# Experts taken in order of load, in steps of one, two or four; shared expert in fp32, fourteen weight buffers, context work moved to layer borders

## The chip, the cores and the metric

One core of one Trainium2 chip runs the whole program as one launch. The metric is the device time of that launch in microseconds (us); smaller is better. The five engines are named as the profile names them: PE (matrix), DVE (vector), ACT (scalar), POOL and SP, the last of which here only issues DMA transfers.

## The reference, cut to what matters

The input x is 256 tokens of 1024 values, batch 1, all in fp32. A first block of two layers (neighbourhood attention with FFN, dilated attention with FFN) is followed by a second block: modulation vectors from `c` and `c_ctx` (called `ada`), a token mixer that also reads 256 context tokens, and a mixture of experts. The change works mostly on the last:

```python
scores = jax.nn.sigmoid(h @ router_w)                  # 256 tokens x 64 experts
...
_, idx = lax.top_k(sel, 8)                             # 8 experts for each token
wts = jnp.take_along_axis(scores, idx, axis=1)
wts = wts / jnp.sum(wts, -1, keepdims=True) * 2.5
...
hid = jax.nn.silu(xb @ w1[e]) * (xb @ w3[e])           # xb: the tokens of expert e
acc.at[tok].add(wt[:, None] * (hid @ w2[e]))
...
shared = (jax.nn.silu(h @ sw1) * (h @ sw3)) @ sw2      # all tokens
```

Each of w1, w3, w2 of an expert is 1024x256 (or 256x1024) in fp32, 1 MiB. There are 64 routed experts and one shared, so 195 MiB of weights if each is read once. The reference's own router, run on the inputs, gives loads (tokens per expert) of 81, 80 and 79 for the three largest and 55 for the next; of the 60 experts after the first four, the 32nd in order of load has 28.

## The kernel before

Up to the mixer, every weight is loaded by `wload` (L387) into a ring of fp32 buffers and split by `wsplit` into a high part `wh` (ACT, L404) and a low part `wl` (DVE, L413). PE then runs three matmuls for one (`yh,wh`, `yl,wh`, `yh,wl`; `proj_a`, `proj_b`). `post` (L548) ends each layer: squares, a sum of squares on PE (`c_base,big 128x1` matmuls), the norm, the residual sum, the next norm. Work on the context tokens and on `ada` is a generator that `beside` sets and `step` advances: the layers call `step` at places written by hand (once per pair of heads, three times at the end of `post`, PS = 3), so that PE gets independent matmuls there. A tile scheduler places all instructions by priority on each engine.

The experts start with `moe` (the shared expert, with split weights and a split input `xh`, `xl`), `route` (scores, top 8, position of each token in its expert's list) and `natural` (tokens turned round). Then `experts` (L2080) takes the routed ones in order of their numbers in pairs. An expert has CAP = 64 slots. One step (a pair) is `moe_in` (w1 in PE's columns 0 to 63 and w3 in 64 to 127 side by side, one expert after the other; 64 tokens `xe` against weights `w`), `moe_out` of the pair before (w2, `w,G`), `moe_slots` (`c_base,oh` and `gate,oh`), a part of the gather for the steps to come (`oh,hnh` and `oh,hnl`), `moe_hidden` and the `scatter` of the pair before (`P,yh` and `P,yl`). Experts with over 64 tokens get further blocks: after step 1, `route_more` counts them, NX = 3 are run after the 64 with weights loaded by an address from a register (`value_load`), and what is still over goes through a loop (`overflow`), which is empty on these inputs. So the kernel loads 3 + 67x3 = 204 MiB here, in 33 pairs and one single step.

The weights come through a ring of `w32` buffers on SP's DMA queue, nine deep from the shared expert on (MW = (9, 4)). A load is issued when its buffer is released by the last matmul that read it; a DMA of SP that waits holds up all behind it. `route_more` issues three of its own on that queue (`scr` twice, `idd`), behind the loads of the third pair.

Of the kernel before, what the change touches and what calls it, by code (L numbers as in the profile page):

```python
# [19 lines left out]
KT = D // 128  # L20
# [7 lines left out]

def _constants():
# [82 lines left out]
    c["ltm"] = lt  # L114
    return {k: np.ascontiguousarray(v, dtype=f) for k, v in c.items()}, mask8
# [3 lines left out]
MOEC = ["iota", "slot", "pidx", "jm", "ltm", "lt8"]  # L119
# [160 lines left out]
class Builder:  # L280
# [267 lines left out]
    def post(self, banks, g, xT, mul=None, perm=None, xnew=None, nxt=None):  # L548
# [20 lines left out]
        self.step(PS)  # L569
        return nxt  # L570

    def out_proj(self, name, oh, ol):
        banks = []
        for j in range(4):
            if j:
# [10 lines left out]
    def na_layer(self, xT, pre, **kw):  # L586
# [6 lines left out]
        for p in range(8):  # L593
            if p % 2 == 0:
# [11 lines left out]
                self.step()  # L606
# [40 lines left out]
        banks = self.out_proj("w_nao", oh, ol)  # L647
        return self.post(banks, self.vec["norm_mix_post0"], xT, **kw)

    def dil_layer(self, xT, pre, **kw):  # L650
# [8 lines left out]
        for p in range(8):  # L659
# [47 lines left out]
            self.step()  # L707
# [38 lines left out]
    def block1(self, xT, xT2, uh, ul):  # L746
# [6 lines left out]
        with self.psum(pc=2, pb=4), self.pool("bp"), self.pool("mp"):  # L753
            with self.pool("ap"), self.pool("lp") as lp:
                pre = self.norm_in(self.vec["norm_mix_pre0"])
                for h in (0, 1):
                    s = slice(4 * h, 4 * h + 4)
                    self.nc.sync.dma_start(xT[:, s, :], self.A["x"][:, s, :])
                    for kt in range(4 * h, 4 * h + 4):
                        pre[2](kt, xT[:, kt, :])  # L760
                self.beside(self.ctx_in(R), lp=lp, bp=None, tags=side)
                pre = self.na_layer(xT, pre, nxt=lambda: self.norm_in(self.vec["norm_ffn_pre0"]))
                self.step(99)
            with self.pool("ap"), self.pool("mr"), self.pool("lp"):
# [3 lines left out]
                pre = self.ffn_layer(xT, 0, pre, perm=(o, i), xnew=xT2, nxt=lambda: self.norm_in(self.vec["norm_mix_pre1"]))  # L768
# [5 lines left out]
            with self.pool("ap"), self.pool("mr"):  # L774
                with self.stream(tc.cur_priority, side):
                    self.load_consts(self.mr, "mixs")
                    self.ssd_ctx(R)
                    self.gla_ctx(R)
                self.ffn_layer(xT2, 1, pre, perm=(i, o), xnew=xT, nxt=lambda: self.ln_in(uh, ul))[3]()
        self.bp = None  # L780

    def ctx_in(self, R):
# [4 lines left out]
        uh, ul = (self.sb(self.lp, [128, KT, 256], t, F32R) for t in ("xh", "ul"))  # L787
        add, sums = self.ln_sums(self.lp, sq="ul")
# [1046 lines left out]
    def route(self, ps):  # L1835
# [47 lines left out]
        nc.vector.tensor_tensor(pos[:, :, 0:64], ps[:, 0:128].rearrange("p (t e) -> p t e", t=2), far, op=OP.add)  # L1883
# [6 lines left out]
        for tt in (0, 1):  # L1890
            nc.vector.tensor_scalar(gate[:, tt, 0:64], sc[:, tt, :], dn[:, 2 + tt:3 + tt], 2.5, op0=OP.mult, op1=OP.mult)
        return sel_

    def route_more(self, sel_):

        nc, mp, c, pos, gate = self.nc, self.mp, self.cst, self.pos, self.gate

        ptf = self.sb(mp, [96, 256], "ptf")
        gtf = self.sb(mp, [96, 256], "gtf")
        for dst, src in ((ptf, pos), (gtf, gate)):  # L1900
            ps = self.pst("pa")
            for tt in (0, 1):
                nc.tensor.transpose(ps[0:64, 128 * tt:128 * tt + 128], src[:, tt, 0:64], self.ident)
            nc.vector.tensor_copy(dst[0:64, :], ps[0:64, 0:256])
        ps = self.pst("pa")
        for tt in (0, 1):
            self.mm(ps[0:64, 0:1], sel_[tt], self.ones[:, 0:1], tt == 0, tt == 1)
        cnt = self.sb(mp, [64, 4], "cnt")
        for b in (1, 2, 3):
            nc.vector.tensor_scalar(cnt[:, b:b + 1], ps[0:64, 0:1], float(b * CAP) + 0.5, None, op0=OP.is_gt)  # L1910
        nc.vector.tensor_tensor(cnt[:, 0:1], cnt[:, 1:2], cnt[:, 2:3], op=OP.add)
        nc.vector.tensor_tensor(cnt[:, 0:1], cnt[:, 0:1], cnt[:, 3:4], op=OP.add)
# [3 lines left out]
        S = self.sb(mp, [64, 32], "S_")  # L1916
        W = self.sb(mp, [64, 32], "W_")
        t = self.sb(mp, [64, 32], "St")
        for b in (1, 2, 3):
            nc.vector.tensor_scalar(pre[:, b:b + 1], ps[0:64, 0:1], float(b - 1), None, op0=OP.add)  # L1920
            d = S if b == 1 else t
            nc.vector.tensor_scalar(d, c["jm"][0:64, :], pre[:, b:b + 1], cnt[:, b:b + 1], op0=OP.is_equal, op1=OP.mult)
            if b == 1:
                nc.vector.tensor_scalar(W, d, float(-CAP) - FAR, None, op0=OP.mult)
            else:
                nc.vector.tensor_tensor(S, S, t, op=OP.add)
                nc.vector.scalar_tensor_tensor(W, t, float(-b * CAP) - FAR, W, op0=OP.mult, op1=OP.add)

# [8 lines left out]
        for tt in (0, 1):  # L1937
            ps = self.pst("pa")
            self.mm(ps[:, 0:32], ptf[0:64, 128 * tt:128 * tt + 128], S, True, False)
            self.mm(ps[:, 0:32], one64, W, False, True)  # L1940
            self.mm(ps[:, 32:64], gtf[0:64, 128 * tt:128 * tt + 128], S, True, True)
            nc.vector.tensor_scalar(pos[:, tt, 64:96], ps[:, 0:32], FAR, None, op0=OP.add)
            nc.vector.tensor_copy(gate[:, tt, 64:96], ps[:, 32:64])
# [3 lines left out]
        nc.vector.tensor_copy(self.ids[:, 0:32], ps[0:1, 0:32])  # L1947
        nc.vector.tensor_scalar(self.ids[:, 32:33], ps[0:1, 32:33], float(-NX), 0.0, op0=OP.add, op1=OP.max)
# [4 lines left out]
    def gather_make(self, pos, n):  # L1953

        o = self.sb(self.gp, [128, 2, 4, CAP], "oh", F32R, bufs=2)
        for tt in (0, 1):
            self.nc.vector.tensor_tensor(o[:, tt, 0:n, :], self.cst["iota"][:, None, :].to_broadcast([128, n, CAP]),
                                         pos[:, tt, :].unsqueeze(2).to_broadcast([128, n, CAP]), op=OP.is_equal)
        return o, self.sb(self.gp, [128, KT, 4 * CAP], "xe", bufs=2)

    def gather_part(self, o, xe, n, q):

        w = CAP * n
        ps = self.pst("pa")
        for k in (0, 1):
            kt = 2 * q + k
            for x, h in enumerate((self.hnh, self.hnl)):
                for tt in (0, 1):
                    self.mm(ps[:, w * k:w * k + w], h[:, tt, 128 * kt:128 * kt + 128],
                            o[:, tt, 0:n, :].rearrange("p e s -> p (e s)"), x == 0 and tt == 0, x == 1 and tt == 1)  # L1970
# [6 lines left out]
    def moe_in(self, xe, i, ws):  # L1977

        pu = self.pst("pa")
        n = len(ws)  # L1980
        for b, (w1, w3) in enumerate(ws):
            o = slice(256 * b, 256 * b + 256)
            for kt in range(KT):
                l = xe[:, kt, CAP * (i + b):CAP * (i + b) + CAP]
                for a, w in ((0, w1), (64, w3)):
                    self.mm(pu[a:a + 64, o], l, w[:, 256 * kt:256 * kt + 256], kt == 0, kt == KT - 1)
# [19 lines left out]
    def moe_out(self, G, ws, gcol):  # L2006

        m = CAP * len(ws)
# [13 lines left out]
    def moe_slots(self, o, i, j, n):  # L2022

        nc = self.nc
        m = CAP * n
        ps = self.pst("pa")
        oh = [o[:, tt, i:i + n, :].rearrange("p e s -> p (e s)").bitcast(F32) for tt in (0, 1)]
        for tt in (0, 1):
            nc.tensor.transpose(ps[0:m, 128 * tt:128 * tt + 128], oh[tt], self.ident)
        for tt in (0, 1):  # L2030
            self.mm(ps[0:m, 256:256 + n], oh[tt], self.gate[:, tt, j:j + n], tt == 0, tt == 1)
        P = self.sb(self.gp, [128, 256], "P_", F32R, bufs=3)
        nc.vector.tensor_copy(P[0:m, :], ps[0:m, 0:256])
        gc = self.sb(self.gp, [128, 3], "gc", bufs=3)
        nc.vector.tensor_tensor_reduce(gc[0:m, 1:1 + n], ps[0:m, 256:256 + n], self.cst["b64"][0:m, 0:64 * n:64],
                                       scale=1.0, scalar=0.0, op0=OP.mult, op1=OP.add, accum_out=gc[0:m, 0:1])
        return P[0:m, :], gc[:, 0:1]
# [15 lines left out]
    def moe(self, hh, hl, acc, after):  # L2053

        nc, A, tc = self.nc, self.A, self.tc
        src = A["w_exp"][0]
        w1, w3, w2 = (self.wsplit(self.wload(src[i]), PSH[i], after, self.lp) for i in range(3))
        pg, pu = self.pst("pa"), self.pst("pa")
        self.proj_a(w1, hh, hl, pg)
        self.proj_a(w3, hh, hl, pu)  # L2060
        f = self.sb(self.gp, [128, 512], "us", bufs=2)
        s = f.rearrange("p (a b) -> p a b", a=2)
        nc.scalar.activation(f, pg, AF.Silu)
        nc.vector.tensor_tensor(f, f, pu, op=OP.mult)
# [243 lines left out]
```

## Time and profile before

| | us |
|---|---|
| median of 3 runs | 2001.54 (1997.59 to 2004.25) |
| the profiled execution: its own time | 2001.76 |
| the profiled execution: its span | 1999.8 |
| two attention layers and their FFNs | 0 to about 1075 |
| `ada`, mixer | about 1090 to 1378 |
| norm, router, shared expert | 1378 to 1433.37 |
| 67 expert blocks in 34 steps | 1433.37 to about 1977.5 |
| last norm and store | to 1999.8 |

The span is the profiled execution's from its first to its last instruction; its own time holds 1.96 us more. PE is busy for 96% of the span, DVE for 48% and ACT for 36%. The stages were read from the first and last instructions of their functions.

### The profile page before, as it was taken

How to read it: one execution, taken by the hardware profiler on the slowest of the kernel's cores; microseconds unless marked ns; L12 is line 12 of the kernel's file. 1: busy time of each engine (PE TensorE's matmuls, PEld its weight loads, DVE VectorE, ACT ScalarE, POOL GpSimd, SP SyncE). 2: the span in 40 equal slices, each digit the busy share in tenths (PEclk: the TensorE clock that was granted, in tenths of full speed). 3: DMA queues.
4: the chain of work that ended last, by engine and by line, in shares of the span. 5: the costliest groups of instructions: out<-in, count | busy, mean ns of one | idle time of the engine just before them, and what ended most of it. 6: DMA issues, size and time to landing. Idle time of an engine off the chain costs nothing. (4 is left out here: it accounts for less than half of the span.)

```text
span 1999.8 us, 40409 instructions
## 1 busy us (share of the span) xinstructions
PE 1912.9 (96%) x17524; PEld 1637.6 (82%) x17524; DVE 957.5 (48%) x1956; ACT 724.6 (36%) x1199; POOL 108.1 (5%) x125
## 2 busy tenths in 40 slices
PE   6999999999999999999997999997999999999997
PEld 6789888899899998789996988776767777777774
DVE  3686565555466566455554775655421222222212
ACT  4354644344444443334444544333311111111112
POOL 0010111000100000100002011101200000000001
PEclk9999999999799999889998999978999999999998
DMA  6644332354444444434543420024589999999992
GB/s 222 219 174 169 126 107 103 112 190 181 156 148 148 169 168 177 176 135 168 188 173 126 154 86 18 23 73 166 228 327 389 400 389 391 392 392 398 392 400 103
DMA packets 62197, 412.72 MB, mean 206 GB/s; under 512 B 7043, under 2 KB 7619, under 8 KB 15555
## 3 DMA queue, kind: packets, MB, share of 16 engines
q1 hardware_dynamic: 62018, 410.13, 54.1%
q8 instruction: 138, 2.26, 0.4%
q14 instruction: 41, 0.33, 0.1%
HBM read 407.94 MB, written 2.16 MB: 205 GB/s over the span
## 5 line engine op out<-in xcount | busy, mean ns | idle before, releaser
L413 DVE TENSOR_TENSOR wl<-w,wh 128x1024 fp32r<-128x1024 f32 x297 | 365.3, 1235 | 220.6 <-ACT wh L404 145.2
L404 ACT ACTIVATE wh<-w 128x1024 fp32r<-128x1024 f32 x302 | 317.5, 1058 | 406.3 <-PE pa L422 215.5
L422 PE MATMUL pa<-big,wh 128*128 128x256 f32 x2432 | 344.7, 288 | 3.4 <-ACT wh L404 2.8
L422 PEld LDWEIGHTS pa<-big,wh 128*128 128x128 f32 x2432 | 312.7, 191 | 12.6 <-issue 3.8
L422 PE MATMUL pa<-w,xe 128*64 128x256 f32 x2144 | 290.7, 383 | 0.0
L422 PEld LDWEIGHTS pa<-w,xe 128*64 128x64 f32 x2144 | 197.5, 137 | 69.4 <-issue 18.5
L522 DVE SCALAR_TENSOR_TENSOR yl<-pa,gc,yh 128x512 fp32r<-128x512 f32 (+1 forms) x68 | 51.0, 750 | 286.3 <-ACT yh L521 286.3
L422 PE MATMUL pa<-big,wl 128*128 128x256 f32 x1216 | 183.7, 286 | 0.0
L422 PE MATMUL pa<-w,G 128*64 128x512 f32 x536 | 166.6, 595 | 0.0
L422 PEld LDWEIGHTS pa<-big,wl 128*128 128x128 f32 x1216 | 160.4, 189 | 3.3 <-issue 1.8
L521 ACT ACTIVATE yh<-pa,gc 128x512 fp32r<-128x512 f32 (+1 forms) x68 | 46.7, 687 | 251.2 <-PE pa L422 251.2
L422 PE MATMUL pa<-wh,big 128*128 128x256 f32 x512 | 103.7, 298 | 0.3 <-ACT big L521 0.3
L422 PE MATMUL pb<-fl,wh 128*128 128x256 f32 x368 | 102.8, 288 | 0.7 <-DVE fl L519 0.7
L422 PE MATMUL pb<-fh,wl 128*128 128x256 f32 x368 | 101.3, 284 | 0.0
L422 PEld LDWEIGHTS pa<-w,G 128*64 128x64 f32 x536 | 51.2, 136 | 60.3 <-issue 55.0
L422 PE MATMUL pb<-fh,wh 128*128 128x256 f32 x368 | 96.2, 291 | 3.2 <-ACT fh L518 3.2
L422 PEld LDWEIGHTS pa<-wh,big 128*128 128x128 f32 x512 | 84.0, 200 | 3.5 <-issue 1.8
L422 PE MATMUL pa<-wl,big 128*128 128x256 f32 x256 | 75.9, 297 | 0.1
L422 PEld LDWEIGHTS pb<-fl,wh 128*128 128x128 f32 x368 | 69.2, 189 | 1.7 <-DVE fl L519 1.1
L422 PEld LDWEIGHTS pb<-fh,wl 128*128 128x128 f32 x368 | 69.5, 189 | 0.3
L422 PEld LDWEIGHTS pb<-fh,wh 128*128 128x128 f32 x368 | 64.7, 189 | 6.1 <-ACT fh L518 4.5
L1989 ACT ACTIVATE us<-pa 128x512 f32<-128x512 f32 (+1 forms) x34 | 20.1, 591 | 128.6 <-PE pa L422 128.6
(956 smaller groups left out, 3302.7 us busy)
## 6 DMA issues: line engine op xcount, KB each, us to landing
w<-in_w_exp_dram SPq DMA_DIRECT2D x204, 1024.0 KB, 9.7
w<-in_w_dqkv_dram SPq DMA_DIRECT2D x36, 1024.0 KB, 4.8
w<-in_w_g_dram SPq DMA_DIRECT2D x22, 1024.0 KB, 4.8
w<-in_w_u_dram SPq DMA_DIRECT2D x22, 1024.0 KB, 4.8
w<-in_w_d_dram SPq DMA_DIRECT2D x22, 1024.0 KB, 4.8
wa<-in_w_ada_dram SPq DMA_DIRECT2D x32, 512.0 KB, 5.7
w<-in_w_inx_dram SPq DMA_DIRECT2D x14, 1024.0 KB, 4.9
w<-in_w_naqkv_dram SPq DMA_DIRECT2D x12, 1024.0 KB, 5.0
```

The source lines that it names most:

```text
L404: i = nc.scalar.activation(wh, s, AF.Copy)
L413: eng.tensor_tensor(wl, s, wh.bitcast(F32), op=OP.subtract)
L422: self.last = self.nc.tensor.matmul(out, l, r, start=start, stop=stop)
L521: nc.scalar.activation(hi, src, AF.Copy, scale=scale)
L522: nc.vector.scalar_tensor_tensor(lo, src, scale, hi.bitcast(F32), op0=OP.mult, op1=OP.subtract)
L1989: self.nc.scalar.activation(us[:, 0:256 * n], pu[:, 0:256 * n], AF.Copy)
```

## The change

- **Plan of steps.** `_plan` builds 25 steps from a string: Q is four experts with 32 slots each, P two with 64, B one with 128 (two blocks of 64 with the same weights). Which experts: the first four by number (NFIX) stay fixed, in two pairs ahead of the plan; `sort` ranks the other 60 by load on chip, and rank decides: the four largest are B, the next 28 P, the 28 smallest Q. Weights of these 60 are loaded by register address, from `eids`, 60 `value_load`s on SP. So 27 steps and 3 + 64x3 = 195 loads, each weight once.
- **Half blocks.** `moe_in` and `moe_out` take 32 slots per expert in a Q, four blocks of 32 columns side by side: 64 matmuls where a pair has 32 of 64 columns, and 16 for 8 in `moe_out`. A B runs its weights twice.
- **Overflow.** `leftover` replaces `route_more`, after step 4 and not after step 1; NX is gone.
- **Shared expert** unsplit: `moe_first` and `moe` in fp32, 32 matmuls of 128x256 and then 16, without `xh`, `xl`, `wsplit`.
- **Ring** of 14 fp32 buffers and no split ones, for the last part, MW = (14, 0).
- **Context work moved.** In the first layer fewer steps (`p < 6`, none in `out_proj`), what is left of `ctx_in` runs in the `post` of the first FFN (`steps=99`); `ada(20, 24)` and the context's part of the GLA mixer (`gla_ctx`) go from the dilated layer and from the second FFN to that FFN's `post`. Smaller: the order of loops in `natural`, banks of `pr` and `pb`, the last sums without a square tile.

```diff
+NFIX = 4
+STEPS = "QPPBQPPBQPPBQPPBQPPQPPQPP"
-MW = (9, 4)
+MW = (14, 0)
...
+    for k in STEPS:
+        n = {"B": 1, "P": 2, "Q": 4}[k]
+        rs = list(range(nxt[k], nxt[k] + n)) * (2 if k == "B" else 1)
+        nxt[k] += n
+        plan.append((k, col, rs))
+        col += len(rs)
...
     def post(self, banks, g, xT, ...
-        self.step(PS)
+        self.step(steps)
...
-        banks = self.out_proj("w_nao", oh, ol)
+        banks = self.out_proj("w_nao", oh, ol, False)
...
-                self.beside(self.ada(8, 24, lp), lp=lp, tags=side)
+                self.beside(self.ada(8, 20, lp), lp=lp, tags=side)
...
+                self.beside(self.late_ctx(R), lp=lp, tags=side)
+                self.ffn_layer(xT2, 1, pre, perm=(i, o), xnew=xT, nxt=lambda: self.ln_in(uh, ul), steps=99)[3]()
...
+    def sort(self, sel_):
...
+        nc.vector.tensor_scalar(kr, kr, cc[:, 1:2], None, op0=OP.is_gt)
+        nc.vector.tensor_reduce(cc[:, 2:3], kr, axis=AX.X, op=OP.add)
...
+        self.mm(ps[0:1, 0:64], c["pidx"][0:64, :], M, True, True)
+        nc.vector.tensor_copy(self.eids, ps[0:1, 0:64])
...
     def moe_in(self, xe, c0, ws, cap=None):
...
-                for a, w in ((0, w1), (64, w3)):
-                    self.mm(pu[a:a + 64, o], l, w[:, 256 * kt:256 * kt + 256], kt == 0, kt == KT - 1)
+                for a in (0, 1):
+                    for y in range(m):
+                        e = m * b + y
+                        s = slice(CAP * a + cap * y, CAP * a + cap * y + cap)
+                        self.mm(pu[s, o], xe[:, kt, c0 + cap * e:c0 + cap * e + cap], ws[e][a][:, 256 * kt:256 * kt + 256], kt == 0, kt == KT - 1)
...
+        w = [self.wload(self.A["w_exp"][0][i]) for i in range(3)]
...
     def experts(self, acc, gather, more):
...
+                        r = nc.sync.value_load(self.eids[0:1, col:col + 1], min_val=0, max_val=NEXP - 1)
...
-            if p == 1:
-                self.route_more(*more)
+            if p == 4:
+                self.leftover(*more)
```

Three places show what stands on an engine now. The first is PE at the border from the first FFN to the dilated layer. Before, the sums of `post` (`c_base,big`) stood between matmuls of the dilated layer's first projections (`wh,big` and `wl,big`, 28 and 14 of them from 520 to 533 us):

```order
L422 MATMUL pa_5802<-wh_5798,big_5718 128x256
L422 MATMUL pa_5802<-wh_5798,big_5719 128x256
L422 MATMUL pb_5721<-c_base_61,big_5720 128x1 x2
L422 MATMUL pa_5802<-wl_5799,big_5718 128x256
L422 MATMUL pa_5802<-wh_5798,big_5718 128x256
L422 MATMUL pa_5872<-wh_5864,big_5718 128x256
```

Now three projections of the context (`pc` banks, `yh,wh`, `yl,wh`, `yh,wl`) stand there, about 130 matmuls in all:

```order
L451 MATMUL pb_5517<-c_base_61,big_5516 128x1 x2
L451 MATMUL pc_5651<-yh_74,wh_5647 128x256
L451 MATMUL pc_5651<-yl_75,wh_5647 128x256
L451 MATMUL pc_5651<-yh_74,wl_5648 128x256 x8
L451 MATMUL pa_5800<-wh_5792,big_5514 128x256
L451 MATMUL pa_5800<-wh_5792,big_5515 128x256
L451 MATMUL pb_5517<-c_base_61,big_5516 128x1 x6
L451 MATMUL pb_5853<-c_base_61,st_c_5850 128x128 x2
L451 MATMUL pc_5718<-yh_74,wh_5710 128x256
L451 MATMUL pc_5718<-yl_75,wh_5710 128x256
```

The dilated layer's own projections begin only at the end of the sums; work on the context has come between.

The second place is SP's queue, where the leftover tokens are written (`w` are weight buffers): the two loads ahead are w1 and w3 of step 5, the first B, and the one behind is its w2.

```order
L418 DMA w_2284_16314<-in_w_exp_dram 128x2048
L418 ISA
L418 DMA w_2285_16316<-in_w_exp_dram 128x2048
L2006 DMA scr<-gtf_15525 32x256
L2005 DMA scr<-ptf_15524 32x256
L2008 DMA idd<-ids_15237 1x33
L418 ISA
L418 DMA w_2295_16378<-in_w_exp_dram 128x2048
```

Before, the same three stood behind the six loads of the third pair (step 2, counted from 0); they now stand three steps later.

The third place is PE at the border from the second FFN to the mixer. Before, after the sums (`lnrow`, `ln_r`, `ln_mr`) the first projection of the mixer (`yh,wh`) followed at once:

```order
L422 MATMUL pb_11580<-lnsq_11579,c_base_61 32x256
L422 MATMUL pb_11623<-c_base_61,lnrow_11621 128x6 x2
L422 MATMUL pb_11635<-c_base_61,ln_r_11628 128x128 x2
L422 MATMUL pb_11635<-c_base_61,ln_mr_11633 128x128 x2
L422 MATMUL pa_11720<-yh_74,wh_11712 128x256
L422 MATMUL pa_11720<-yl_75,wh_11712 128x256
```

Now four pieces of `ada` (`w,cs` and `adar`) stand between:

```order
L451 MATMUL pb_11616<-c_base_61,lnrow_11614 128x6 x2
L451 MATMUL pc_11540<-gv_2209,gle_11532 128x256
L451 MATMUL pc_11546<-w_1559_11547,cs_242 32x256 x8
L451 MATMUL pb_11628<-c_base_61,ln_r_11621 128x128 x2
L451 MATMUL pb_11628<-c_base_61,ln_mr_11626 128x128 x2
L451 MATMUL pc_11559<-c_base_61,adar_11557 128x2 x2
L451 MATMUL pc_11563<-w_1563_11564,cs_242 32x256 x8
L451 MATMUL pc_11576<-c_base_61,adar_11574 128x2 x2
L451 MATMUL pc_11580<-w_1567_11581,cs_242 32x256 x8
L451 MATMUL pc_11593<-c_base_61,adar_11591 128x2 x2
L451 MATMUL pc_11597<-w_1571_11598,cs_242 32x256 x8
L451 MATMUL pa_11714<-yh_74,wh_11706 128x256
```

Work that ran beside earlier layers now fills the place between the norm's sums and the projection.

## Rows read from the trace of the kernel before


**Rows 1.** The page: busy time by engine and the 40 slices.

```profile
PE 1912.9 (96%) x17524; PEld 1637.6 (82%) x17524; DVE 957.5 (48%) x1956; ACT 724.6 (36%) x1199; POOL 108.1 (5%) x125
...
PEclk9999999999799999889998999978999999999998
...
GB/s 222 219 174 169 126 107 103 112 190 181 156 148 148 169 168 177 176 135 168 188 173 126 154 86 18 23 73 166 228 327 389 400 389 391 392 392 398 392 400 103
```

**Rows 2.** Busy by stretch: five engines (instructions), granted clock, DMA share, GB/s.

```profile
1500.00:1600.00 100.00, 100.00 (x757) 72.32 (x756) 20.97 (x49) 17.81 (x31) 0.00 (x0) 1.00 0.98 395
1600.00:1700.00 100.00, 100.00 (x767) 74.09 (x767) 20.46 (x49) 17.29 (x31) 0.00 (x0) 1.00 0.98 390
1900.00:1950.00 50.00, 50.00 (x382) 36.57 (x382) 9.61 (x23) 8.55 (x15) 0.00 (x0) 1.00 0.99 399
```

**Rows 3.** Groups by shape, 1500 to 1900 us.

```profile
L422 PE MATMUL pa<-w,xe 128*64 128x256 f32 x1600 | 219.9, 381 | 0.0
...
L422 PE MATMUL pa<-w,G 128*64 128x512 f32 x400 | 126.7, 595 | 0.0
...
L1989 ACT ACTIVATE us<-pa 128x512 f32<-128x512 f32 x25 | 14.9, 597 | 70.4 <-PE pa L422 70.4
```

**Rows 4.** What SP's DMA queue waited for, 1380 to 1980 us.

```profile
SPq L389 <- PE pa L422: 433.4, 100, 19.6
...
SPq L1950 <- DVE ptf L1933: 11.1, 1, 11.1
```

**Rows 5.** DMA issues: KB each, median us from issue to landing.

```profile
w<-in_w_exp_dram SPq DMA_DIRECT2D x204, 1024.0 KB, 9.7
w<-in_w_dqkv_dram SPq DMA_DIRECT2D x36, 1024.0 KB, 4.8
```

**Rows 6.** Busy by stretch: before the experts, early in them, late in them.

```profile
1390.00:1400.00 10.00, 7.42 (x35) 7.14 (x36) 8.34 (x20) 7.47 (x19) 3.66 (x5) 0.50 1.02 430
1460.00:1470.00 10.00, 7.32 (x36) 4.76 (x38) 3.91 (x25) 0.00 (x0) 0.00 (x0) 0.71 0.31 107
1940.00:1950.00 10.00, 10.00 (x83) 8.06 (x81) 2.23 (x6) 2.11 (x4) 0.00 (x0) 1.00 1.01 421
```

**Rows 7.** Timeline of PE: shared expert, first routed matmul, last expert's down projection.

```profile
1430.54 0.28 PE L422 MATMUL pb<-fl,wh 128*128 128x256 f32 x1
1430.66 0.28 PE L422 MATMUL pb<-fh,wl 128*128 128x256 f32 x1
...
1433.37 1.08 PE L422 MATMUL pa<-w,xe 128*64 128x256 f32 x8
...
1972.62 3.65 PE L422 MATMUL pa<-w,G 128*64 128x512 f32 x8
```

**Rows 8.** Groups by shape, 1380 to 1437 us (router, shared expert).

```profile
L422 PE MATMUL pa<-xl,wh 128*128 128x256 f32 x32 | 10.0, 332 | 1.0 <-POOL xl L2200 1.0
...
L422 PE MATMUL pa<-rep,c_moe 128*128 128x64 f32 x4 | 0.8, 280 | 3.6 <-issue 3.6
```

**Rows 9.** Timeline of PE: blocks of 32 columns.

```profile
1370.02 0.40 PE L422 MATMUL pa<-xT,lnw 128*32 128x256 f32 x1
...
1370.04 0.40 PE L422 MATMUL pa<-md,lnw 128*32 128x256 f32 x1
1370.26 0.38 PE L422 MATMUL pa<-xT,lnw 128*32 128x256 f32 x1
```

**Rows 10.** Busy time by stretch at two layer borders.

```profile
510.00:520.00 10.00, 8.30 (x55) 4.39 (x55) 6.39 (x15) 4.14 (x9) 4.03 (x4) 0.67 0.78 264
520.00:533.00 13.00, 13.00 (x64) 13.00 (x64) 6.98 (x13) 5.33 (x13) 3.60 (x3) 0.52 0.21 81
...
1080.00:1090.00 10.00, 6.45 (x39) 2.85 (x39) 5.44 (x17) 3.11 (x8) 5.37 (x7) 0.73 0.55 210
1090.00:1100.00 10.00, 6.17 (x24) 4.66 (x25) 7.32 (x16) 6.54 (x15) 4.65 (x6) 0.61 0.08 16
```

**Rows 11.** Timeline of PE at the border before the mixer.

```profile
1094.36 0.58 PE L422 MATMUL pa<-yh,wh 128*128 128x256 f32 x1 [3.36 <-ACT yh L518]
```

More of the change, by code (lines that the diff above doesn't have):

```diff
@@ L27, with _plan @@
 NEG = -1e30
+def _plan():
+    nxt = {"B": NFIX}
+    nxt["P"] = NFIX + STEPS.count("B")
+    nxt["Q"] = nxt["P"] + 2 * STEPS.count("P")
+    plan, col = [], 0
+    for k in STEPS:
[4 more added lines that the diff above has]
+        col += len(rs)
+    return plan
 def _constants():
@@ L760, in block1 @@
                         pre[2](kt, xT[:, kt, :])
-                self.beside(self.ctx_in(R), lp=lp, bp=None, tags=side)
+                self.beside(self.ctx_in(R, uh, ul), lp=lp, bp=None, tags=side)
                 pre = self.na_layer(xT, pre, nxt=lambda: self.norm_in(self.vec["norm_ffn_pre0"]))
-                self.step(99)
             with self.pool("ap"), self.pool("mr"), self.pool("lp"):
@@ L786, in ctx_in @@
         self.nc.sync.dma_start(xc, self.A["ctx"])
-        uh, ul = (self.sb(self.lp, [128, KT, 256], t, F32R) for t in ("xh", "ul"))
-        add, sums = self.ln_sums(self.lp, sq="ul")
+        add, sums = self.ln_sums(self.lp)
         for kt in range(KT):
@@ L1905, in route_more @@
         ps = self.pst("pa")
         for tt in (0, 1):
[L1907 to L1912, printed above, removed]
+            self.mm(ps[:, 64 * tt:64 * tt + 64], ptf[0:64, 128 * tt:128 * tt + 128], M, True, True)
@@ L2108, in experts @@
             with self.behind(whole):
                 halves = []
-                if p < len(pairs):
-                    us = self.moe_in(g[bi][1], i, [(self.wload(v[0]), self.wload(v[1])) for v in src])
+                if p < len(steps):
+                    w = {b: (self.wload(v[0]), self.wload(v[1])) for b, v in src.items()}
+                    us = self.moe_in(g[bi][1], 128 * i, [w[b] for b in blocks], cap)
                     halves.append(self.last)
                 if prev is not None:
-                    prev["y"] = self.moe_out(prev["G"], prev["w"], prev["gc"])
+                    prev["y"] = self.moe_out(prev["G"], prev["w"], prev["gc"], prev["cap"])
@@ L2198, in tail @@
                             nc.scalar.activation(hf[:, kt, :], t, AF.Identity, bias=mod(3)(kt))
-                            last.append(nc.scalar.activation(hh[:, kt, :], hf[:, kt, :], AF.Copy))
-                            PL(nc, kt).tensor_tensor(hl[:, kt, :], hf[:, kt, :], hh[:, kt, :].bitcast(F32), op=OP.subtract)
                             add3(kt, hf[:, kt, :])
                     self.natural(hf)
+                    w, pg, first = self.moe_first()
+                    for kt in range(KT):
+                        first(kt, hf[:, kt, :])
                     acc = [self.pst("pb") for _ in range(4)]
-                    self.moe(hh, hl, acc, last[LG])
+                    self.moe(pg, w, acc)
                     with tc.high_priority(offset=HR):
-                        more = (self.route(logits),)
-                    gather = self.gather_make(self.pos[:, :, 0:4], 4)
+                        sel = self.route(logits)
+                    gather = self.gather_make((self.pos[:, :, 0:NFIX], CAP))
                     for q in range(KT // 2):
-                        self.gather_part(*gather, 4, q)
+                        self.gather_part(*gather, q)
+                    with tc.high_priority(offset=HR):
+                        more = self.sort(sel)
                     ab = self.sb(self.lp, [128, KT], "ab")
```

288 lines of the change are left out of this document (164 added, 124 removed).

## The prediction

> **What bounds it now.** I read the page first: PE is busy for 96% of the span, and only in the nine slices before the last do the transfers move 389 to 400 GB/s, where all earlier ones have 18 to 327 [rows 1]. So one stretch has two candidates for its limit, and the question is which one ends last there. The busy times by stretch put PE at 100.00 of 100 us at the full granted clock, and DMA at a share of 0.98 to 0.99 at 390 to 399 GB/s [rows 2]. A share near 1 does not make DMA the pace, since queued packets count as busy; the rate tells more. In other stretches the same share goes with 430 and 421 GB/s [rows 6], so up to a tenth is left. And the wait of the queue that issues the loads settles it: 433.4 us, 100 times, for a buffer that PE still reads [rows 4]. PE sets the pace, but with little to spare.
>
> In 1500 to 1900 us one row stands once per pair, 25 times [rows 3], so a pair takes 400/25 = 16.0 us. In that time 6 MiB are loaded, 16.0/6 = 2.67 us per MiB, which is the 393 GB/s seen. The 64 + 3 blocks take 33.5 such pairs, from the first routed matmul at 1433.37 to the last down projection at 1972.62 [rows 7].
>
> **The steps on PE.** 27 steps take the place of 34. A P is a pair as before. A B has the same matmuls as a pair with one expert's weights. A Q has twice the matmuls of `moe_in` and `moe_out`, each of 32 columns. What four such blocks side by side cost is seen in the sums of the norm: the first and the fourth start 0.02 us apart, the fifth 0.22 us after the fourth [rows 9]. So four run at once where two of 64 columns do, and a Q takes a pair's 16.0 us. If Q's did not overlap at all beyond two, `moe_in` and `moe_out` would double, and those two hold about 10.7 of the 16 us by matmuls that run in twos (219.9 and 126.7 us for 25 pairs, overlapping, [rows 3]); I take the row that shows it, 16.0. PE then needs 27 x 16.0 = 432 us, against 539 us (1433.37 to 1972.62).
>
> **The loads.** 192 MiB of routed weights must come in, in place of 201. The four fixed ones (12 loads) and the shared three come before the first step, as nine loads do now, so 180 are left. The time of one is bounded by the rates above: 2.44 us at 430 GB/s and 2.49 at 421 [rows 6], 2.63 at 399 and 2.69 at 390 [rows 2], the last two while PE paced. I take 2.60, near the slowest row that is not PE's whole pace. 180 x 2.60 = 468 us (439 to 484). This is more than PE's 432: **DMA becomes the bound**. It shows by kind of step: a cycle QPPB loads 12 + 6 + 6 + 3 = 27 MiB, 70.2 us, and gives PE 64; QPP loads 24, 62.4 us, and gives PE 48. So the seven fewer steps (107 us) are worth about 60. Loads by a register's address cost nothing extra by what is seen: the nine such loads of before come last of all, where 421 GB/s were reached [rows 6].
>
> **The start.** The first routed matmul is at 1433.37 [rows 7]. The shared expert in fp32 has 48 matmuls of two passes; a pass of 256 columns holds its columns for 0.22 us [rows 9], so 96 x 0.22 = 21 us in place of 144 split matmuls that start 0.12 apart [rows 7], 17: +4. `sort` adds some 14 small matmuls, about +2.5. What goes is waiting: 1.0 us for the split input, 3.6 us ahead of the routing's sums, when DVE and POOL share their time with splits [rows 8]. So 1433.4 + 6.5 - 4.6 = 1435 (1431 to 1440). In the meantime the queue has its 14 buffers full, and it goes on when the shared expert's and the first step's buffers come free and `eids` is read: 1437.
>
> **The stall of the leftovers.** `route_more` now holds the queue for 11.1 us [rows 4], and the rate falls to 107 GB/s in the ten us around it [rows 6]. `leftover` has the same form, three steps later, with 26 loads of the 180 ahead of it on the queue. They have landed at about 1437 + 2 + 26 x 2.60 = 1507; `leftover`'s results come after step 4, 1435 + 5 x 16 = 1515. Between nothing (PE a little earlier) and 12 us I take 6.
>
> **The end.** First transfer: a load that waits for nothing takes 4.8 us to land [rows 5], 2.2 beside its 2.60. Last landing: 1437 + 2.2 + 468 + 6 = 1913. Behind it stands the last down projection with all that follows, now 1972.62 to 1999.8, 27.2 us [rows 7], and for two experts and not one another 3: 1943 of span. With 2.0 us around it (2001.76 less 1999.8) 1945.
>
> **The borders.** The work that moves is the same; it is worth what PE loses there now. In 510 to 533 PE idles 1.7 us and has a mean granted clock of 0.67 and 0.52: two thirds of 10 us and 12.5 of 13 at 1.2 GHz, half of which is lost, some 11 us with the idle time. In 1080 to 1100 it is 7.4 us idle and, by 0.73 and 0.61, 6.6 us of clock [rows 10], 3.36 of it a single wait for the split input of the mixer [rows 11]. Filling takes a matmul that is ready. At the first border those are three projections of context, some 130 matmuls of 0.12 us, 16 us of dense work; I take 9 of the 11. At the second the filling is small matmuls, and their weights go through the same ring ahead of the mixer's first ones, so the mixer may start some 3 us later; I take 6 net. Together -15 (+3 to -25). The stretches they left keep their pace: there PE has enough ready work.
>
> **Clock.** With DMA the pace, PE waits. The stretch that shows what a wait costs has 2.7 us idle in 10 and then a granted clock of 0.71, 5.8 us at 1.2 GHz, 2.9 lost [rows 6]. While PE has 36 us to spare (468 less 432) most of that is covered, but not in the last step and the tail. +8. The sum: 1945 - 15 + 8 = **1938**, 64 us below the profiled 2001.76, which is 0.2 above the median of 2001.54.
>
> **A rule that speaks against.** The Trainium skill, "TensorE: Matmul & The Clock Gate", section "HAM oscillation — how this bites in real kernels", says that a kernel whose matmuls wait for a transfer at each step of a loop starts each of them at the low clock. The stretch at 1460 agrees for one wait. By the rule it would be every waiting step, which is the second case below. The "HBM Reference" of the Trainium skill, "Specifications (TRN2)", gives a core about 358 GB/s when its neighbour streams too and 425 alone. By 358 a load would take 2.93 us and the sum would be 1997; by 425, 2.47 us and 1915. Only one core runs here, and the rows with 390 to 430 lie above the first.
>
> **The rivals.**
> - *DMA paces as worked out*: 1938, chance 0.58. For it: the queue's wait would go, the rates exist.
> - *The half clock makes PE the bound*: 4 cycles with two waits and 9 steps with one are 17 waits, 17 x 2.9 = 49 us, or 73 if all 25 steps wait. PE would need 481 to 505 against 468: 13 to 37 us more, about 1958. Against it: such waits need a PE that is ahead, so they stop when it is late. 0.15. Q's that take 7 us longer come out there too (7 x 7 = 49).
> - *The borders give nothing*, since the new filling is no denser than the old: 1953, 0.13.
> - *Loads reach 2.50 us*: 18 us less, 1920. The floor is PE's 432 us. 0.07.
> - *Slower or no gain*: 60 reads of a list by SP and 180 addresses from registers hold the queue up. Against it the 421 GB/s. It takes 2.96 us per load for no gain (64/180 = 0.36 more) and 2.99 for 6 us slower, which is 0.3% and about what can be told from no change. 0.03 for the same, 0.04 for slower.
>
> **The range.** The cases reach from 1920 to 1958; with the bounds of the start (5), the stall (6) and the borders (10) it is 1915 to 1968, and 0.07 to 0.1 lie on each side. Faster 0.93, same 0.03, slower 0.04.
>
> **What the profile after would show.** The queue's wait for PE falls from 433 us to under 150, and PE has idle time ahead of `w,xe`, released by DMA, 20 to 60 us in all, most of it in Q's and in the last three cycles; steady rates of 395 to 420 GB/s. First routed matmul 1420 (1435 less the borders). Q's `moe_in` within 10% of a P's. Granted clock in 510 to 533 above 0.8. Wrong would be: PE still at 100 of 100 us (then blocks of 32 columns don't run four at once, or the clock fell), a load at over 2.7 us while PE waits, or the same losses at the borders in other places.

## The result and the profile after

The changed kernel takes 1927.74 us (median of 4 runs, 1925.52 to 1930.25) where before takes 2001.03 in the same comparison: a ratio of 0.9639, 95% interval 0.9616 to 0.9663, 72 us (67 to 77). The forecast was 1938, 10 us above, range 1915 to 1968. The profiled execution took 1925.83 us with a span of 1924.1.

The page of the changed kernel, the same three lines as [rows 1]:

```profile
PE 1819.9 (95%) x17242; PEld 1529.2 (79%) x17242; DVE 926.4 (48%) x1935; ACT 699.9 (36%) x1154; POOL 95.3 (5%) x112
...
PEclk9999999999999999989999899999899999999898
...
GB/s 227 220 176 169 112 88 96 137 189 184 121 166 149 168 174 178 163 143 154 183 190 132 207 116 82 24 27 90 195 348 388 301 421 420 420 421 420 421 420 148
```

PE is busy for 95% of a shorter span. The transfers now hold 420 and 421 GB/s in slices 32 to 38 (counted from 0), where before had 389 to 400; one slice ahead of them (31) falls to 301. The busy times by stretch tell why; columns as in [rows 2], the stretches answer to [rows 6] and [rows 10]:

```profile
510.00:520.00 10.00, 7.94 (x47) 7.68 (x48) 6.27 (x10) 2.62 (x6) 0.23 (x1) 0.66 0.57 196
520.00:533.00 13.00, 13.00 (x113) 13.00 (x112) 6.79 (x9) 7.74 (x12) 0.00 (x0) 1.00 0.50 173
1080.00:1090.00 10.00, 7.33 (x41) 5.97 (x42) 5.76 (x12) 4.35 (x9) 0.77 (x1) 0.50 0.66 240
1090.00:1100.00 10.00, 10.00 (x84) 10.00 (x84) 7.05 (x10) 4.71 (x6) 0.00 (x0) 0.98 0.82 318
1390.00:1400.00 10.00, 10.00 (x61) 9.09 (x60) 5.85 (x30) 6.94 (x13) 0.00 (x0) 1.00 1.01 423
...
1480.00:1490.00 10.00, 10.00 (x81) 6.97 (x78) 1.58 (x3) 1.98 (x3) 0.00 (x0) 1.00 0.76 314
1490.00:1500.00 10.00, 7.33 (x49) 5.12 (x49) 4.64 (x22) 0.88 (x2) 0.00 (x0) 0.83 0.00 0
1500.00:1510.00 10.00, 10.00 (x67) 5.50 (x68) 1.17 (x2) 0.69 (x1) 0.00 (x0) 0.83 0.62 215
1600.00:1700.00 100.00, 100.00 (x890) 65.02 (x885) 20.40 (x54) 16.97 (x30) 0.00 (x0) 1.00 1.01 420
```

Three things stand here. In a steady stretch (1600 to 1700) the rate is 420 GB/s, 2.49 to 2.50 us for each MiB, with PE at 100% as well. In 1480 to 1510 the transfers stop: against 420 GB/s these 30 us lose 106, 420 and 205 GB/s of ten us each, 17 us of transfers. And in 1390 to 1400 the clock is 1.00, where before had 0.50 [rows 6]; but the same work stands 9.6 us earlier here (the sums of the norm ahead of it start at 1371.00, before at 1380.60), so the stretch is compared from its own start, with `b_shared` below.

What SP's queue waited for in the experts (answers to [rows 4]), and what PE waited for there:

```profile
SPq L418 <- DMA w<-in_w_exp_dram: 217.9, 122, 3.5
SPq L418 <- PE pa L451: 95.2, 46, 8.4
SPq L2006 <- DVE ids L2003: 27.7, 1, 27.7
...
SPq L2185 <- DVE eids L1955: 13.0, 1, 13.0
```

```profile
PE pa L451 <- DMA w<-in_w_exp_dram: 17.9, 8, 3.9
PE pa L451 <- DVE S__2273_16253 L1990: 2.7, 1, 2.7
```

The waits for PE have gone from 433.4 to 95.2 us. The largest sum is now the wait for an earlier transfer, 217.9 us: the transfers are full. The leftovers hold the queue for 27.7 us (11.1 before); their first write and the next load of a weight are issued at:

```profile
1499.47 0.37 SPq L2006 DMA_DIRECT2D scr<-gtf  x1
...
1502.47 9.10 SPq L418 DMA_DIRECT2D w<-in_w_exp_dram  x10
```

PE waits for loads 17.9 us, 8 times. The first routed matmul and the last down projection, as in [rows 7]:

```profile
1418.61 1.73 PE L451 MATMUL pa<-w,xe 128*64 128x256 f32 x14
...
1897.00 3.65 PE L451 MATMUL pa<-w,G 128*64 128x512 f32 x16
```

The first is 14.8 us earlier, and the stretch between them is 478.4 us, 60.9 less than before. The end is 27.1 us behind the second, as it was.

In steady steps, a copy by ACT ends each step's `moe_in`. Five of them, of a Q, P, P, B and the next Q:

```profile
1607.05 0.60 ACT L2054 ACTIVATE us<-pa 128x512 f32<-128x512 f32 x1 [6.40 <-PE pa L451]
...
1624.36 0.60 ACT L2054 ACTIVATE us<-pa 128x512 f32<-128x512 f32 x1 [2.84 <-PE pa L451]
...
1640.45 0.60 ACT L2054 ACTIVATE us<-pa 128x512 f32<-128x512 f32 x1 [2.82 <-PE pa L451]
...
1656.04 0.60 ACT L2054 ACTIVATE us<-pa 128x512 f32<-128x512 f32 x1 [7.54 <-PE pa L451]
...
1674.24 0.60 ACT L2054 ACTIVATE us<-pa 128x512 f32<-128x512 f32 x1 [6.40 <-PE pa L451]
```

From one to the next it is 17.31, 16.09, 15.59 and 18.2 us: the cycle of four takes 67.2 us, and 27 loads of 2.49 take 67.2 as well. Only the two steps around the Q are longer than 16.1. The matmuls of the P behind the Q of these rows show why; `w,xe` is its `moe_in`, `w,G` 32 columns wide is the Q's down projection:

```profile
1611.93 0.65 PE L451 MATMUL pa<-w,xe 128*64 128x256 f32 x2
1612.51 1.90 PE L451 MATMUL pa<-w,G 128*32 128x512 f32 x10
1614.34 3.67 PE L451 MATMUL pa<-w,xe 128*64 128x256 f32 x32
1617.95 2.77 PE L451 MATMUL pa<-w,G 128*32 128x512 f32 x22
1620.65 3.67 PE L451 MATMUL pa<-w,xe 128*64 128x256 f32 x30
1624.25 0.44 PE L2096 MATMUL pa<-c_base,oh 128*128 128x128 f32 x2
```

The two are interleaved in the program. A matmul is two records. From start to start, the single one of `w,xe` takes 0.58 us and sixteen in a row 3.61, 0.23 each; five of `w,G` (four and one) take 1.83, 0.37 each, and the other eleven 2.70, 0.25 each. These times fit 0.9 us for each four of `w,G` that are begun (two of them 1.83, three 2.70), so a run that ends within a four seems to leave the other columns empty; in the same way the last fifteen of `w,xe` take 3.60 us, as long as sixteen. The change of width itself costs little by these rows. The busy time of `moe_in` alone does not show it. In the cycle from 1594.17 to 1661.37 the three steps of P and B have the first row, 8.4 us each, and the Q the second:

```profile
L451 PE MATMUL pa<-w,xe 128*64 128x256 f32 x192 | 25.2, 382 | 0.0
...
L451 PE MATMUL pa<-w,xe 128*32 128x256 f32 x129 | 8.7, 380 | 0.0
```

### The profile page after: what moved, and what is told of

It reads as the page before. It is cut to its first block, busy times and chain, and to the rows that moved or that the text cites. A ratio compares the mean times of both kernels' runs of the same rounds, so it can differ in the third digit from the quotient of the medians.

```text
span 1924.1 us, 40201 instructions
## 1 busy us (share of the span) xinstructions
PE 1819.9 (95%) x17242; PEld 1529.2 (79%) x17242; DVE 926.4 (48%) x1935; ACT 699.9 (36%) x1154; POOL 95.3 (5%) x112
## 5 line engine op out<-in xcount | busy, mean ns | idle before, releaser
L433 ACT ACTIVATE wh<-w 128x1024 fp32r<-128x1024 f32 x296 | 311.4, 1058 | 420.9 <-PE pa L451 206.0
L442 DVE TENSOR_TENSOR wl<-w,wh 128x1024 fp32r<-128x1024 f32 x296 | 360.0, 1224 | 210.3 <-ACT wh L433 122.5
L451 PE MATMUL pa<-w,xe 128*64 128x256 f32 (+1 forms) x2176 | 230.5, 392 | 18.0 <-DMA w<-in_w_exp_dram 17.9
L451 PEld LDWEIGHTS pa<-w,xe 128*64 128x64 f32 (+1 forms) x2176 | 137.9, 129 | 107.7 <-issue 41.0
L551 DVE SCALAR_TENSOR_TENSOR yl<-pa,gc,yh 128x512 fp32r<-128x512 f32 x54 | 40.5, 751 | 213.6 <-ACT yh L550 213.6
L451 PE MATMUL pa<-w,G 128*64 128x512 f32 (+1 forms) x544 | 129.5, 616 | 0.0
L550 ACT ACTIVATE yh<-pa,gc 128x512 fp32r<-128x512 f32 x54 | 37.1, 688 | 210.3 <-PE pa L451 210.3
L451 PE MATMUL pb<-fh,wh 128*128 128x256 f32 x352 | 91.1, 289 | 0.9 <-ACT fh L547 0.9
L451 PEld LDWEIGHTS pa<-w,G 128*64 128x64 f32 (+1 forms) x544 | 35.1, 127 | 61.4 <-issue 59.6
L2054 ACT ACTIVATE us<-pa 128x512 f32<-128x512 f32 x27 | 16.1, 597 | 141.4 <-PE pa L451 132.0
```

The costliest lines, as they stand in the source:

```text
L433: i = nc.scalar.activation(wh, s, AF.Copy)
L442: eng.tensor_tensor(wl, s, wh.bitcast(F32), op=OP.subtract)
L451: self.last = self.nc.tensor.matmul(out, l, r, start=start, stop=stop)
L550: nc.scalar.activation(hi, src, AF.Copy, scale=scale)
L551: nc.vector.scalar_tensor_tensor(lo, src, scale, hi.bitcast(F32), op0=OP.mult, op1=OP.subtract)
L2054: self.nc.scalar.activation(us[:, 0:256 * n], pu[:, 0:256 * n], AF.Copy)
```

## The experiments

The theory after the result: (1) what the experts gain comes from seven steps fewer on PE, until the loads are the limit, at 2.49 us each; borders and shared expert give the rest. Rivals: the fewer loads or the deeper ring give it; PE still sets the end.

**Steps of four taken out** (`a_pairs`): 34 steps, the same 195 loads.

```diff
-STEPS = "QPPBQPPBQPPBQPPBQPPQPPQPP"
+STEPS = "PPPPPPPBPPPPPPPBPPPPPPPBPPPPPPPB"
```

> The changed kernel with no step of four: 4 double blocks and 28 pairs, 34 steps with the fixed ones, still 195 loads. Theory 1 (the gain of the experts comes from fewer steps on PE, until the loads are the limit): PE paces again at 16.0 us per step, 34 x 16.0 = 544 us where the changed kernel has 482 from the first routed matmul to the last down projection, so some 1985 to 1995 us. Theory 2 (it comes from 9 loads fewer and the deeper ring): it stays within 15 us of 1928.

Measured 1990.85 us, ratio 0.9962 (0.9942 to 0.9983). Nearly all of the gain is gone. SP's queue waits for PE again:

```profile
SPq L418 <- PE pa L451: 290.0, 81, 9.6
```

So neither the nine loads fewer nor the ring of 14 gives it without the steps of four; of the 72 us, 64 hang on them.

**Without w3** (`a_w1_only`): the routed experts' w3 is left out, w1 stands in both halves, 128 loads in place of 192, all matmuls kept.

```diff
-                    w = {b: (self.wload(v[0]), self.wload(v[1])) for b, v in src.items()}
+                    w = {b: (self.wload(v[0]),) * 2 for b, v in src.items()}
```

> The changed kernel without the routed experts' w3: w1 stands in both halves, so 128 loads in place of 192 and the same instructions on PE; the output lacks the w3 product. Theory 1 (in the cycle of QPPB, 67.2 us, the loads and PE are equal: a Q costs PE about 19 us and not 16): the steps keep their times, only the 18 us of PE's waits for loads and part of the stall of the leftovers go, 1900 to 1910 us. Theory 2 (the loads alone pace, PE needs 16.0 us for every step): a cycle falls from 67.2 to 64 us, a QPP to 48, and the time to about 1880 us.

Measured 1869.92 us, ratio 0.9354 (0.9323 to 0.9384). The time is nearer to the second theory, but the steps are shorter than either had them. The copies that end `moe_in`, of two P, a B and a Q:

```profile
1599.85 0.60 ACT L2054 ACTIVATE us<-pa 128x512 f32<-128x512 f32 x1 [8.58 <-PE pa L451]
...
1615.53 0.60 ACT L2054 ACTIVATE us<-pa 128x512 f32<-128x512 f32 x1 [8.58 <-PE pa L451]
...
1631.09 0.60 ACT L2054 ACTIVATE us<-pa 128x512 f32<-128x512 f32 x1 [8.58 <-PE pa L451]
...
1646.67 0.60 ACT L2054 ACTIVATE us<-pa 128x512 f32<-128x512 f32 x1 [8.61 <-PE pa L451]
```

All are 15.6 apart, Q or not. In this kernel the program's order differs: `moe_in` stands in one piece ahead of the down projection (64 records of `w,xe` from 1608.30, then 16 of `w,G` from 1615.26). That led to a third theory, that a Q costs PE more only through the interleaving; it is tried below. With a third of the loads gone PE waits for none, and the time is 58 us below the changed kernel's; fewer loads and shorter steps are both in that number.

**Leftovers on another queue** (`a_left_pool`): three transfers issued by POOL.

```diff
-        nc.sync.dma_start(self.scr[0], ptf[64:96, :])
-        nc.sync.dma_start(self.scr[1], gtf[64:96, :])
+        nc.gpsimd.dma_start(self.scr[0], ptf[64:96, :])
+        nc.gpsimd.dma_start(self.scr[1], gtf[64:96, :])
...
-        nc.sync.dma_start(self.idd, self.ids)
+        nc.gpsimd.dma_start(self.idd, self.ids)
```

> The changed kernel with the three transfers of the leftovers issued by POOL, so that the queue of the weights does not wait for them. Theory 1 (the loads set the end of the experts): the gap of 16 us without transfers in 1488 to 1504 goes, and most of it from the time, 1912 to 1918 us. Rival (PE sets the end, the gap is made good): 1923 to 1928 us.

Measured 1915.41 us, ratio 0.9579 (0.9554 to 0.9604), below the changed kernel's interval by itself. The stretch of the gap:

```profile
1480.00:1490.00 10.00, 10.00 (x83) 7.56 (x80) 2.00 (x5) 1.64 (x3) 0.00 (x0) 1.00 1.01 420
1490.00:1500.00 10.00, 7.34 (x43) 4.33 (x41) 4.21 (x19) 0.88 (x2) 1.18 (x2) 0.78 1.02 423
1500.00:1510.00 10.00, 10.00 (x73) 6.14 (x74) 1.17 (x2) 0.69 (x1) 0.57 (x2) 0.88 1.01 419
```

The gap is gone, and some 12 of its 17 us with it: what the transfers lose is for the most part in the time, so the loads set the end.

**Nine buffers** (`a_ring9`):

```diff
-MW = (14, 0)
+MW = (9, 0)
```

> The changed kernel with 9 weight buffers in place of 14. Theory 1 (the loads pace, and a Q takes 12 at once): with fewer than 12 buffers the queue waits for PE in every Q, 10 Q and B transitions with 1 to 4 us each, 1940 to 1965 us. Rival (the depth does nothing since the rate is the limit): within 5 us of 1928.

Measured 1958.82 us, ratio 0.9808 (0.9772 to 0.9844), 31 us above 14 buffers. SP's queue waits for PE 317.3 us in place of 95.2, and PE for loads 40.1 us, 13 times, in place of 17.9:

```profile
PE pa L451 <- DMA w<-in_w_exp_dram: 40.1, 13, 5.3
```

With the steps of four, the depth is needed, since the queue must run ahead of a step that takes twelve buffers.

**The borders alone, in the kernel before** (`b_borders`): all edits of the context work (`steps=99`, `late_ctx`, `ada(8, 20)`, `p < 6`), as in the diff of the change, nothing else.

```diff
-                pre = self.ffn_layer(xT, 0, pre, perm=(o, i), xnew=xT2, nxt=lambda: self.norm_in(self.vec["norm_mix_pre1"]))
+                pre = self.ffn_layer(xT, 0, pre, perm=(o, i), xnew=xT2, nxt=lambda: self.norm_in(self.vec["norm_mix_pre1"]), steps=99)
...
+                self.beside(self.late_ctx(R), lp=lp, tags=side)
```

> The kernel before with the context work moved to the layer borders and nothing else of the change. The two traces put 9.6 us of the gain ahead of the norm that starts the last part. Theory 1 (the borders give that by themselves): 1990 to 1993 us where before has 2001, 8 us of it by the end of the dilated layer, 2 at the second border. Rival (part of it comes from elsewhere, the border work only moves): 1997 to 2001 us.

Measured 1993.55 us, ratio 0.9961 (0.9944 to 0.9979): 8 us (4 to 11). The stretches of [rows 10]:

```profile
520.00:533.00 13.00, 13.00 (x112) 13.00 (x111) 6.87 (x9) 7.62 (x12) 0.00 (x0) 1.00 0.45 163
1090.00:1100.00 10.00, 10.00 (x85) 10.00 (x84) 7.15 (x10) 4.42 (x6) 0.00 (x0) 0.99 0.81 306
```

From 520 on the clock is 1.00 where it was 0.52, and from 1090 on 0.99 where it was 0.61. Ahead of both the low clock remains, as in the changed kernel's rows above (0.66 and 0.50).

**The first border alone** (`b_border1`): as in `b_borders`, but without `late_ctx`, `ada(8, 20)` and `p > 1`.

```diff
+                pre = self.ffn_layer(xT, 0, pre, perm=(o, i), xnew=xT2, nxt=lambda: self.norm_in(self.vec["norm_mix_pre1"]), steps=99)
...
                 self.beside(self.ada(8, 24, lp), lp=lp, tags=side)
```

> The kernel before with the first border alone: fewer steps of the context in the first layer and the rest at the end of the first FFN; the modulation and the GLA context stay where they were. Theory 1 (nearly all of the borders' gain is the first one): 1990 to 1994 us, as with both. Rival (each border gives about half, as the prediction's 9 and 6 had it): 1995 to 1997 us.

Measured 1997.80 us, ratio 0.9992 (0.9973 to 1.0011). Its profiled execution, 1990.62 us, is the fastest of 12 that reach up to 2005.93, so its trace is no guide. The interval rules out the first theory's 8 us and reaches the rival's. How the 8 us divide stays open.

**The shared expert alone, in the kernel before** (`b_shared`): `moe_first`, `moe`, the loop order of `natural` and the banks of `pr` and `pb`; the ring keeps nine fp32 buffers and loses the split ones (MW = (9, 0)).

```diff
+                    w, pg, first = self.moe_first()
+                    for kt in range(KT):
+                        first(kt, hf[:, kt, :])
                     acc = [self.pst("pb") for _ in range(4)]
-                    self.moe(hh, hl, acc, last[LG])
+                    self.moe(pg, w, acc)
```

> The kernel before with the shared expert unsplit in fp32 and nothing else of the change. Theory 1 (the splits on ACT, DVE and POOL, not PE, set the length of this stretch, and its half clock goes with the waits): the first routed matmul comes 8 to 12 us earlier and the time falls by as much, 1990 to 1994 us, more than the 5 us that remain in the changed kernel, which also sorts. Rival (PE's own matmuls set it, as the prediction summed it): within 3 us of 2001 or slower.

Measured 1994.25 us, ratio 0.9969 (0.9948 to 0.9989): 6 us (2 to 10), the first theory's sign, at the low end of its size. The stretch from the sums of the norm (`c_base,lnrow`) to the first routed matmul, in the kernel before, here, and in the changed kernel:

```profile
1380.60:1433.37 52.77, 40.30 (x250) 37.99 (x250) 35.02 (x105) 22.02 (x41) 20.02 (x18) 0.77 0.59 239
1378.56:1424.80 46.24, 37.93 (x202) 33.41 (x202) 26.98 (x102) 13.62 (x26) 3.44 (x5) 0.85 0.62 251
1371.00:1418.61 47.61, 39.92 (x225) 35.00 (x225) 28.31 (x113) 14.98 (x29) 3.45 (x5) 0.86 0.80 331
```

It is 6.5 us shorter than before. PE idles 8.3 us of it in place of 12.5, and is busy 37.9 us in place of 40.3, at a mean clock of 0.85 in place of 0.77. The half clock does not go at once: 10 to 20 us behind the norm's sums it is 0.57 (0.50 before), in the next ten 1.00 (0.72 before). The first routed matmul is 8.6 us earlier, but 2 us of that lie ahead of the norm, where nothing was changed.

**The down projection first** (`a_out_first`): in each step `moe_out` of the step before stands ahead of `moe_in`, in one piece.

```diff
+                if prev is not None:
+                    prev["y"] = self.moe_out(prev["G"], prev["w"], prev["gc"], prev["cap"])
+                    halves.append(self.last)
                 if p < len(steps):
                     w = {b: (self.wload(v[0]), self.wload(v[1])) for b, v in src.items()}
-                    us = self.moe_in(g[bi][1], 128 * i, [w[b] for b in blocks], cap)
-                    halves.append(self.last)
-                if prev is not None:
-                    prev["y"] = self.moe_out(prev["G"], prev["w"], prev["gc"], prev["cap"])
+                    with self.behind(halves):
+                        us = self.moe_in(g[bi][1], 128 * i, [w[b] for b in blocks], cap)
```

> The changed kernel with the down projection of the step before put ahead of each step's first matmuls, so that the two are not interleaved on PE. Theory 1 (blocks of 32 columns cost PE 3 us more per step of four only because they are interleaved with blocks of 64): all steps without a wait take 15.6 us, waits for the loads take the place of what is saved, and since the loads set the end in most of it, 1918 to 1926 us. Rival (a step of four needs the 19 us by itself, and the equal steps of the kernel without w3 come from reading the same weights twice): 17.4 and 17.8 us beside each Q as before, 1928 us.

Measured 1922.46 us, ratio 0.9598 (0.9568 to 0.9627), which overlaps the changed kernel's. The time alone does not decide it; the steps do, shown with `a_both`.

**Both, with the steps reordered** (`a_best`): the last two edits, and each Q at the end of its cycle.

```diff
-STEPS = "QPPBQPPBQPPBQPPBQPPQPPQPP"
+STEPS = "PPBQPPBQPPBQPPBQPPQPPQPPQ"
```

> Both together, the transfers of the leftovers on POOL's queue and the down projection first, with each step of four at the end of its cycle, so that the last step is a Q. Theory 1 (then nothing but the loads is left, 180 x 2.49 us from the first by address): 1900 to 1908 us. Rival (the gains overlap): 1912 to 1916 us as with the first alone.

Measured 1920.14 us, ratio 0.9588 (0.9560 to 0.9615), above the rival's range too: worse than `a_left_pool` by its median. The rows of the start tell of a gap of another kind:

```profile
1490.00:1500.00 10.00, 7.34 (x43) 4.19 (x44) 4.38 (x20) 0.88 (x2) 1.23 (x2) 0.86 0.54 199
1500.00:1510.00 10.00, 10.00 (x134) 4.72 (x134) 1.66 (x3) 1.37 (x2) 0.52 (x1) 0.97 0.46 154
```

P, P, B ask for 15 MiB in three steps, 37 us of transfers, while PE takes 47 us for them and then works for the leftovers; the 14 buffers are full, and the queue waits for PE (38.1 us in 1470 to 1520, 13.0 at the longest), though the leftovers' transfers no longer hold it. What is not transferred then is missing at the end.

**Both, in the order of the change** (`a_both`): `a_left_pool` and `a_out_first` together.

> The changed kernel with the transfers of the leftovers on POOL's queue and the down projection first, its own order of steps kept. Theory 1 (the other order, with the light steps first, cost the earlier kernel with both its gain, since the ring filled while PE paced and the queue stood still for 11 us): at the limit of the loads, 1908 to 1914 us, no worse than POOL's queue alone. Rival (the down projection first costs what it saves once the loads run without a gap): 1916 to 1921 us as with the other order.

Measured 1908.89 us, ratio 0.9551 (0.9528 to 0.9575), the fastest here, 19 us below the changed kernel; its interval meets that of `a_left_pool`. The copies that end `moe_in`, of a B, a Q, two P and a B:

```profile
1576.18 0.60 ACT L2054 ACTIVATE us<-pa 128x512 f32<-128x512 f32 x1 [6.28 <-PE pa L451]
...
1591.94 0.60 ACT L2054 ACTIVATE us<-pa 128x512 f32<-128x512 f32 x1 [6.51 <-PE pa L451]
...
1607.59 0.60 ACT L2054 ACTIVATE us<-pa 128x512 f32<-128x512 f32 x1 [6.39 <-PE pa L451]
...
1623.14 0.60 ACT L2054 ACTIVATE us<-pa 128x512 f32<-128x512 f32 x1 [6.28 <-PE pa L451]
...
1638.69 0.60 ACT L2054 ACTIVATE us<-pa 128x512 f32<-128x512 f32 x1 [6.28 <-PE pa L451]
```

They are 15.76, 15.65, 15.55 and 15.55 us apart: with different weights for w1 and w3, and Q's in one piece, a Q costs PE what a pair does. So the 17.3 and 18.2 us were the interleaving, and not the reading of one weight twice. `a_w1_only` has such steps too and takes 39 us less with a third of the loads gone: the loads are the limit here as well. The transfers have no gap left where the leftovers stood:

```profile
1500.00:1600.00 100.00, 100.00 (x910) 64.70 (x909) 21.94 (x57) 17.50 (x31) 1.75 (x3) 0.98 1.01 420
```

## Why the prediction was right, and where it was off

- *What bounds it now, and the change of the bound*: as said, but with less between the two limits: a cycle takes 67.2 us on either, where 70.2 for the loads and 64 for PE were said. `a_pairs` shows that the steps on PE were the limit, `a_left_pool` that a gap in the loads is in the time now, `a_both` beside `a_w1_only` that the loads are the limit once the steps are in one piece. "DMA paces as worked out" was the case that came.
- *The steps on PE, 16.0 us for a Q*: wrong for this program. Blocks of 32 columns do run four at once, as [rows 9] had it, but interleaved with blocks of 64 a Q makes a cycle 3 us longer (67.2 for 64). The forecast that Q's `moe_in` is within 10% of a P's held by busy time (8.7 and 8.4 us), and so was no sign of it: the price lies where the two widths cut each other's runs. It cost little, as the loads take the same 67.2 us for the cycle.
- *The loads, 2.60 us*: mis-sized. 2.49 us, 180 x 0.11 = 20 us less than taken. The row of 421 GB/s was the one to take; those of 399 and 390 were PE's pace after all. The "HBM Reference" of the Trainium skill, "Specifications (TRN2)", has 425 GB/s for a core alone, which this trace's 420 supports; 358 would have been wrong.
- *The stall of the leftovers, 6 us*: mis-sized the other way, 17 us. The first result came when it was said: its write is issued 80.9 us behind the first routed matmul, where 80 was taken. The loads ahead had landed some 12 us before that; the forecast had 8 between the two (1507 and 1515) and took 6, and faster loads (26 x 0.11 = 3 us) make up most of the difference. The term had nothing for what follows: 3.0 us until the writes are issued and the queue has its next load (1499.47 to 1502.47), and some 2 more until the rate is back. The terms of the loads and of the stall hid each other.
- *The start*: the first routed matmul is 5.2 us earlier by the last part alone (14.8 less the 9.6 by which the sums of the norm ahead of it come earlier), where +1.6 was said. The waiting went as forecast, 4.8 us for 4.6 (12.5 idle before, 7.7 now). The step that failed is PE's own work, +6.5 with the sort: PE is busy 0.4 us less. The fp32 matmuls take what was said (the last 32 passes 7.2 us), but the work they replace was counted at the full clock, 0.12 us for a split matmul, and in that stretch the clock was 0.77 in the mean; now it is 0.86. Why it rises earlier was not tried by itself. The stretch hardly scatters from trace to trace: 52.8 us in before and in `b_borders`, 47.6 in the changed kernel and in `a_left_pool`.
- *The borders, -15*: 8 us (4 to 11) by `b_borders`, within the bounds of the prediction but half of its value. What goes is the low clock of 520 to 533 and 1090 to 1100; what was counted as lost in 510 to 520 and 1080 to 1090 remains (clock 0.66 and 0.50, 2.1 and 2.7 us idle in the changed kernel).
- *Clock, +8*: nothing of it is seen in the sum, although the clock did fall. PE waits for loads at six places. Behind four of them it is low (0.54 in 1544 to 1548, 0.51 in 1793 to 1797, 0.77 in 1805 to 1809, 0.50 in 1853 to 1857), behind the other two (from 1529 and from 1865 on) it is 1.00. The rule of the Trainium skill, "TensorE: Matmul & The Clock Gate", section "HAM oscillation — how this bites in real kernels", would have had each waiting step start at the low clock; four of these six agree. The transfers kept 414 to 426 GB/s in all these stretches, so the low clock cost the loads nothing.
- *The end*: 27.1 us behind the last down projection, as taken. But the last load lands at about 1892, 5 us ahead of that matmul, and PE's last wait for a load ends at 1865.68: the last steps are PE's. From the landing to the end it is 32 us, where 30 were taken, and the last loads come at a falling rate (50 GB/s in 1890 to 1900), some 2 us more.

In the sum of the profiled executions: 1938, borders +5, start -7, loads -20, stall +11 and clock -8 make 1919; 1925.83 was measured. Some 4 of the 7 us left are those of the end, the others the roughness of these terms. Besides the gap of the leftovers the transfers have none: the rate is 417 to 425 GB/s in every ten us from 1430 to 1480 and from 1510 to 1880. So the mechanism was right, and that the sum came within 12 us is in part luck: errors of 20, 8 and 7 us one way met 11, 5 and 7 us the other. The first routed matmul, forecast for 1420 and found at 1418.61, is luck too: the borders gave 5 us less and the start 7 us more. Of the other signs, the queue's wait for PE (95.2 us, under 150) and the clock in 510 to 533 (0.85, above 0.8) came; PE's wait for loads, 17.9 us, lies just under the 20 to 60 forecast.

## What to carry to other kernels

Where an engine is at 100% and the transfers near it, work out both limits for each kind of step: a change that relieves the one is worth only the distance to the other, and then every gap of the transfers is in the time, whichever transfer on the queue makes it. Take the rate of a transfer from the stretch with the most in flight, not from one that an engine paces. Keep the matmuls of narrow column blocks in one piece, a multiple of four, uncut by wider ones.

## What was not expected of the hardware

- Interleaved runs of 32 and 64 columns cost 3.2 us per Q (67.2 us for a cycle of four, where four steps of 16.0 are 64), and in one piece next to nothing (15.65 and 15.76 beside 15.55). By the rows of the P behind a Q (1.83 us for five, 2.70 for eleven), a run that ends on the first of four takes nearly what four take.
- A pair in one piece also gains a little: 15.55 in place of 16.0 us.
- The same program's executions differ: twelve of `b_border1` reach from 1990.62 to 2005.93 us, so a difference of 10 us between two traces early in the program shows nothing by itself.
